# Row-by-row ReLU and row sums rewritten with own semaphores, wide instructions in six blocks, and both stores on one queue

## The chip, the cores and the metric

The kernel runs on one core of one Trainium2 chip. Its time is the device time of one execution in microseconds (us), and medians and means are over executions in the fast state only (all runs here were, or were single looks whose state is called unknown). Each execution also lists the span of the core: from the first to the last instruction of the program that the profile records. The time is longer than the span. The difference I call the *time outside the span*. The run lists give spans to 0.1 us, so a time outside taken from them is good to 0.05 us.

## The reference

```python
# x: float32 [32, 512, 1024]
relu_x = np.maximum(x, 0)
return np.sum(relu_x, axis=-1)        # [32, 512]
```

There are 16,384 rows of 1024 numbers (67.11 MB). Each is clamped at zero and summed, so almost all that moves is the input.

## The kernel before

Each of the 128 partitions owns 128 rows. Seven loads bring 16 rows each, then loads of 8, 4, 2 and 1 rows follow, and the last row comes in four pieces so that little work is left after the last byte. Rows alternate between ScalarE (ReLU with an accumulator) and VectorE (max with zero, then add). The 16-row and 8-row tiles share two buffers. A framework places the semaphores and waits.

```python
chunks = [16] * 7 + [8, 4, 2, 1]            # pieces = [244, 252, 260, 268]
io_pool = ctx.enter_context(tc.tile_pool(name="io", bufs=2))
...
for j, cpd in enumerate(chunks):
    ...                                     # tile xt of cpd rows
    nc.sync.dma_start(out=xt, in_=xv[...])
    for c in range(cpd):
        m = m0 + c
        if m == NT - 2:
            act_op(xt[:, c, :], xt[:, c, :], m)
            nc.scalar.dma_start(out=out2d[:, 0 : NT - 2], in_=res[:, 0 : NT - 2])   # store 1
        elif (c % 2) == 0:
            act_op(xt[:, c, :], xt[:, c, :], m)
        else:
            dve_op(xt[:, c, :], xt[:, c, :], res[:, m : m + 1])
...                                         # four pieces on VectorE
nc.sync.dma_start(out=out2d[:, NT - 2 : NT], in_=res[:, NT - 2 : NT])              # store 2
```

Of the kernel before, what the change touches and what calls it, by code (L numbers as in the profile page):

```python
# [1 line left out]

# [4 lines left out]



EARLY = 1  # L10


def kernel(tc: tile.TileContext, x: bass.AP, out: bass.AP):
    trace_relu_sum(tc, x, out)
    tc.close()
    tc.compile()  # L16
    issue_ahead_of_the_barrier(tc, EARLY)


def issue_ahead_of_the_barrier(tc: tile.TileContext, n_loads: int):  # L20


    SP = mybir.EngineType.SP
    blocks = tc.nc.main_func.blocks
    opening = blocks[0].instructions
    body = next(b for b in blocks if b.name == tc.start_bb_name).instructions
    loads = [i for i in body if i.engine == SP][:n_loads]
    for i in loads:
        assert isinstance(i, mybir.InstDMACopy)
        body.remove(i)  # L30
    at = next(
        n
        for n, i in enumerate(opening)
        if i.engine == SP and isinstance(i, mybir.InstDrain)
    )
    opening[at:at] = loads


@with_exitstack
def trace_relu_sum(  # L40
    ctx: ExitStack,
    tc: tile.TileContext,
    x: bass.AP,
    out: bass.AP,
):
    nc = tc.nc
    fp32 = mybir.dt.float32

    P = nc.NUM_PARTITIONS
    x_flat = x.flatten_outer_dims()  # L50
    N, D = x_flat.shape
    assert N % P == 0
    NT = N // P

    xv = x_flat.rearrange("(p m) d -> p (m d)", p=P)
    out2d = out.rearrange("b s -> (b s)").rearrange("(p m) -> p m", p=P)

    big = 16
    tail = [8, 4, 2, 1]
    pieces = [244, 252, 260, 268]  # L60
    assert sum(pieces) == D
    nbig, rem = divmod(NT - sum(tail) - 1, big)
    assert rem == 0
    chunks = [big] * nbig + tail

    io_pool = ctx.enter_context(tc.tile_pool(name="io", bufs=2))
    res_pool = ctx.enter_context(tc.tile_pool(name="res", bufs=1))
    res = res_pool.tile([P, NT], fp32)

    def act_op(in_ap, out_ap, m):  # L70
        nc.scalar.activation(  # L71
            out=out_ap,
            in_=in_ap,
            func=mybir.ActivationFunctionType.Relu,
            accum_out=res[:, m : m + 1],
        )

    def dve_op(in_ap, out_ap, accum_out):
        nc.vector.tensor_scalar(  # L79
            out=out_ap,  # L80
            in0=in_ap,
            scalar1=0.0,
            scalar2=None,
            op0=mybir.AluOpType.max,
            op1=mybir.AluOpType.add,
            accum_out=accum_out,
        )

    m0 = 0
    for j, cpd in enumerate(chunks):  # L90
        if cpd >= 8:
            xt = io_pool.tile([P, cpd, D], fp32, tag="io", name=f"xt{j}")
        else:
            xt = io_pool.tile([P, cpd, D], fp32, tag=f"t{cpd}", bufs=1, name=f"xt{j}")
        nc.sync.dma_start(  # L95
            out=xt,
            in_=xv[:, m0 * D : (m0 + cpd) * D].rearrange("p (c d) -> p c d", c=cpd),
        )
        for c in range(cpd):
            m = m0 + c  # L100
            if m == NT - 2:
                act_op(xt[:, c, :], xt[:, c, :], m)
                nc.scalar.dma_start(out=out2d[:, 0 : NT - 2], in_=res[:, 0 : NT - 2])
            elif (c % 2) == 0:
                act_op(xt[:, c, :], xt[:, c, :], m)
            else:
                dve_op(xt[:, c, :], xt[:, c, :], res[:, m : m + 1])
        m0 += cpd

    m_last = m0  # L110
    assert m_last == NT - 1
    base = m_last * D
    np_ = len(pieces)
    wlast = pieces[-1] + (np_ - 1)
    ptiles = []
    col = 0
    for i, w in enumerate(pieces):
        shape_w = w if i < np_ - 1 else wlast
        pt = io_pool.tile([P, shape_w], fp32, tag=f"p{i}", bufs=1, name=f"p{i}")
        ptiles.append(pt)  # L120
        nc.sync.dma_start(out=pt[:, 0:w], in_=xv[:, base + col : base + col + w])
        col += w
    last = ptiles[-1]
    for i in range(np_ - 1):
        dve_op(ptiles[i], ptiles[i], last[:, pieces[-1] + i : pieces[-1] + i + 1])
    dve_op(last, last, res[:, m_last : m_last + 1])

    nc.sync.dma_start(out=out2d[:, NT - 2 : NT], in_=res[:, NT - 2 : NT])


# [1 line left out]
_INS = ['x']  # L132
_OUTS = [((32, 512), 'float32')]


# [23 lines left out]
```

## Time and profile before

| what | value | where it is read |
|---|---|---|
| median time, 3 runs | 163.64 us (163.27 to 163.69) | run list |
| span of the profiled run, its time | 161.5 us, 163.31 us | run list |
| load queue, share of 16 DMA engines | 96.9% | page, part 3 |
| VectorE, ScalarE busy | 46%, 43% | page, part 1 |

These are lines of the page of the kernel before, parts 1 and 3. Part 1 gives busy time, share of the span and number of instructions; part 3 gives packets, megabytes and the share of the sixteen DMA engines' span for each queue.

```profile
span 161.5 us, 347 instructions
DVE 74.3 (46%) x134; ACT 69.0 (43%) x129; POOL 0.2 (0%) x4
...
q1 hardware_dynamic: 2304, 67.11, 96.9%
q10 hardware_dynamic: 144, 0.06, 0.1%
q14 instruction: 2, 0.02, 0.0%
```

The load queue q1 is busy almost all of the time and the compute engines are not half busy, so the kernel is bound by the input stream. The queue q10 is ScalarE's store queue.

This is the chain of waits of the kernel before (start, length, what).

```profile
0.78 40.80 DMA xt<-in_x_dram
41.59 0.02 issue
41.61 9.22 DVE xt L79 x16
50.83 0.02 SPq L95
50.85 0.03 issue
50.88 29.41 DMA xt<-in_x_dram
```

The chain seems to say that 9.22 us of VectorE work stand between loads. They do not: the load issued at about 50.9 us queues up behind another one, which is still running and lands only at 60.93 us. A chain follows releases, and a release that comes early is shown all the same. That no time is lost is shown by the landings below, 19.35 us apart.

The end of the kernel before, from the timeline of VectorE and SyncE (start, length, engine, line, operation):

```profile
157.58 0.41 DVE L79 TENSOR_SCALAR_CACHE_REDUCE p<-p 128x244 f32<-128x244 f32 x1 [0.40 <-DMA p<-in_x_dram]
...
158.74 0.43 DVE L79 TENSOR_SCALAR_CACHE_REDUCE p<-p 128x271 f32<-128x271 f32 x1
159.10 0.08 DVE L79 DVE_READ_ACCUMULATOR p<-p 128x1 f32 x1
159.25 0.35 SPq L128 DMA_DIRECT2D out_dram<-res  x1
```

The last piece is reduced at 158.74 us, and store 2 is issued at 159.25 us; the span ends at 161.52 us.

A load is done when all sixteen DMA engines have landed their sixteenth of it. The trace has these landings one by one. The next table is worked out from them, in us; the two 8 KiB instruction packets are at 86.35 and 86.65 us.

| load (before) | first engine | last but one | last |
|---|---|---|---|
| third, 16 rows | 59.97 | 60.84 | 60.93 |
| fourth, 16 rows | 79.35 | 80.20 | 80.29 |
| fifth, 16 rows | 98.70 | 99.63 | 100.13 |
| last piece | 157.27 | 158.12 | 158.60 |

Up to the fourth load the last engine trails the next by 0.09 us. From the fifth on, the first after the instruction packets, it trails by 0.49 us, and keeps this up to the last piece.

### The profile page before, as it was taken

To read this page: it belongs to the slowest core of one execution; us is meant where nothing else is said; L and a number is where in the kernel's file an instruction comes from. 1 tells how busy PE (TensorE), PEld (TensorE's weight loads), DVE (VectorE), ACT (ScalarE), POOL (GpSimd) and SP (SyncE) were. 2 spreads that over 40 slices of the span, in tenths; PEclk is the share of its full clock that TensorE was granted. 3 is DMA by queue.
4 is the path that set the end of the run, shared out by engine and by line. 5 is a ranking of instruction groups with operands and counts; after the bars stand their busy time and mean duration, and the time that the engine had idled before them with its cause. 6 is when DMAs were issued, how large, how long until landed. Compare 5 with 4: busy or idle time off the path is not lost.

```text
span 161.5 us, 347 instructions
## 1 busy us (share of the span) xinstructions
DVE 74.3 (46%) x134; ACT 69.0 (43%) x129; POOL 0.2 (0%) x4
## 2 busy tenths in 40 slices
DVE  0000049700695008940099101991039900598983
ACT  3000049500693008920099001990039700596882
POOL 0000000000000000000000000000000000000000
DMA  8997997996997997997996997997997997999990
GB/s 308 471 503 308 487 487 308 503 503 292 503 503 308 487 503 325 471 519 308 471 519 296 487 503 325 471 503 341 454 503 341 454 503 308 430 438 406 406 359 22
DMA packets 2450, 67.19 MB, mean 416 GB/s; under 512 B 528, under 2 KB 1040, under 8 KB 1168
## 3 DMA queue, kind: packets, MB, share of 16 engines
q1 hardware_dynamic: 2304, 67.11, 96.9%
q10 hardware_dynamic: 144, 0.06, 0.1%
q14 instruction: 2, 0.02, 0.0%
HBM read 67.11 MB, written 0.07 MB: 416 GB/s over the span
## 4 chain that ended last, share of the span: by engine, by line
DMA 79%; DVE 18%; SPq 1%; issue 0%; DVEq 0%
DMA xt<-in_x_dram 62%; DVE xt L79 17%; DMA p<-in_x_dram 17%; SPq L95 1%; DVE p L79 1%; DVEq L79 0%; DVEq L16 0%
## 5 line engine op out<-in xcount | busy, mean ns | idle before, releaser
L79 DVE TENSOR_SCALAR_CACHE_REDUCE xt<-xt 128x1024 f32<-128x1024 f32 x63 | 72.6, 1216 | 84.5 <-DMA xt<-in_x_dram 84.2
L71 ACT ACTIVATE xt<-xt 128x1024 f32<-128x1024 f32 x64 | 66.7, 1043 | 89.0 <-DMA xt<-in_x_dram 89.0
L71 ACT ACTIVATION_READ_ACCUMULATOR xt<-xt 128x1 f32 x64 | 11.9, 187 | 0.0
L79 DVE DVE_READ_ACCUMULATOR xt<-xt 128x1 f32 x63 | 5.2, 83 | 0.0
L79 DVE TENSOR_SCALAR_CACHE_REDUCE p<-p 128x244 f32<-128x244 f32 (+3 forms) x4 | 1.6, 420 | 0.4 <-DMA p<-in_x_dram 0.4
L71 ACT ACT_TABLE_LOAD x1 | 1.3, 1283 | 0.8 <-PEq L143 0.8
L79 DVE DVE_READ_ACCUMULATOR p<-p 128x1 f32 x4 | 0.3, 82 | 0.0
L143 POOL MEMSET const-bfloat16-1.0<- 128x1 bf16 x1 | 0.1, 101 | 0.0
L143 POOL MEMSET const-uint8-127<- 128x1 uint8 x1 | 0.1, 101 | 0.0
L143 POOL MEMSET const-float32-0.0<- 128x1 f32 x1 | 0.1, 98 | 0.2 <-issue 0.2
L143 POOL MEMSET const-float32-1.0<- 128x1 f32 x1 | 0.1, 98 | 0.0
## 6 DMA issues: line engine op xcount, KB each, us to landing
xt<-in_x_dram SPq DMA_DIRECT2D x1, 4096.0 KB, 19.6
xt<-in_x_dram SPq DMA_DIRECT2D x1, 2048.0 KB, 24.2
xt<-in_x_dram SPq DMA_DIRECT2D x1, 1024.0 KB, 26.2
xt<-in_x_dram SPq DMA_DIRECT2D x1, 512.0 KB, 27.0
p<-in_x_dram SPq DMA_DIRECT2D x1, 134.0 KB, 10.0
p<-in_x_dram SPq DMA_DIRECT2D x1, 130.0 KB, 26.5
p<-in_x_dram SPq DMA_DIRECT2D x1, 126.0 KB, 26.7
p<-in_x_dram SPq DMA_DIRECT2D x1, 122.0 KB, 26.8
```

What stands on the lines that cost most here:

```text
L71: nc.scalar.activation(out=out_ap, in_=in_ap, func=mybir.ActivationFunctionType.Relu, accum_out=res[:, m : m + 1],)
L79: nc.vector.tensor_scalar(out=out_ap, in0=in_ap, scalar1=0.0, scalar2=None, op0=mybir.AluOpType.max, op1=mybir.AluOpType.add, accum_out=ac ...
L95: nc.sync.dma_start(out=xt, in_=xv[:, m0 * D : (m0 + cpd) * D].rearrange("p (c d) -> p c d", c=cpd),)
L143: nc = _bacc.Bacc("TRN2", target_bir_lowering=False, num_devices=1)
```

## The change

Its intent: fewer instructions and fewer waits, a deeper queue of loads, and a shorter end. In six of the seven 16-row blocks ScalarE now clamps up to 16 rows in one instruction and VectorE sums them in one. There are three 16-row buffers. The last block and the tail stay row by row. Both stores go out on SyncE's queue. The wait for the last store is put into the closing block, behind the branch to it. The core of the diff (the load, the row instructions, the tail and the pieces are left out):

```diff
-    io_pool = ctx.enter_context(tc.tile_pool(name="io", bufs=2))
+NBUF = 3
+TWO = [[16], [16], [16], [8, 8], [8, 8], [6, 5], []]
+ACT = [0, 0, 0, 0, 0, 5, 8]
+DVE = [0, 0, 0, 0, 0, 0, 8]
...
+    def clamp(ap, loaded):
+        i = nc.scalar.activation(out=ap, in_=ap, func=RELU)
+        ...                                          # waits for its load
+        i.then_inc(sems.act, 1)
+    def total(ap, m, n):
+        nc.vector.tensor_reduce(
+            out=res[:, m : m + n], in_=ap, axis=mybir.AxisListType.X, op=ADD
+        ).wait_op(sems.act, n_act, "sem-ge").then_inc(sems.dve, 1)
...
+        for n in TWO[j]:
+            clamp(buf[:, c : c + n, :], act_waits)
+            total(buf[:, c : c + n, :], m + c, n)
...
-                nc.scalar.dma_start(out=out2d[:, 0 : NT - 2], in_=res[:, 0 : NT - 2])
+    store(0, NT - 2, n_act - 1, n_dve)               # on nc.sync
...
+    nc.cur_bb = nc.bb_map[tc.start_bb_name + "_end"] # the closing block
+    nc.sync.wait_ge(sems.stored, 16 * n_stores)
```

## The prediction

> **What bounds the kernel now.** The input stream. The page gives 67.11 MB read in a span of 161.5 us, the load queue's packets taking 96.9% of the sixteen DMA engines' span, while VectorE is busy 46% and ScalarE 43%. The trace's DMA records show 64 KiB packets of 2.418 us each, back to back: 16 x 65,536 B / 2.418 us = 434 GB/s, which is the 435 GB/s fabric ceiling of the Trainium skill ("DMA: Bandwidth & Descriptors", Where 436 GB/s comes from). Every 16-row load after the first lands 19.35 us after the one before. The chain of waits shows 9.22 us VectorE stretches, but the queue still holds the next load then (a load is issued at 50.8 us; the one before it lands at 60.9), so they cost nothing. Two buffers never starve the queue.
>
> **What the change does to the middle: nothing for time.** From the durations of before (1,039 ns per 1024-element ACTIVATE; VectorE 1,216 ns at 1024 and 414 ns near 257 elements, so about 1.05 ns per element) I estimate 13.8 us for a 16-row clamp and 17.3 us for a 16-row reduce. VectorE is the busiest engine at 17.3 < 19.35 us per load. A buffer comes free about 31 us after landing; with three buffers its next load is needed about 38 us after landing, 7 us of slack. Busy shares rise (VectorE to about 75%, ScalarE to about 65%), the stream stays at 434 GB/s. The last block and the tail are row by row as before.
>
> **What can move: under 1 us.**
> 1. Instruction fetch. The trace shows two 8 KiB packets on the instruction queue at 86.35 and 86.65 us (16 KiB, the block of 256 instructions of the Trainium skill, "Runtime: NRT & Kernel Launch", Instruction fetch mechanics). They hold up one DMA engine: it lands 1.3 us later from then on and becomes the last. Before the fetch the last engine trails the next by 0.09 us, after it by 0.49 us, up to the last piece. Both compute streams are then about 64 records in; the changed ones have about 50 to 60 records in all, against 147 and 143. I expect no fetch in the stream: last landing about 0.48 us earlier.
> 2. The last store is issued at 159.25 us, its wait ends near 160.6, the closing barrier runs 160.8 to 161.5. With the wait behind the branch, the branch hides under the store: 0.1 to 0.2 us.
> 3. Store 1 moves from ScalarE's queue to SyncE's, behind the loads. It needs 0.37 us of issue at about 157.2 us; SyncE is free until 159. Nothing on the critical path.
> 4. VectorE's end (four piece instructions, 157.58 to 159.18) stays.
>
> Sum: about -0.6 us of 163.64 us, all at the end, so I predict 163.0 us, with 162.3 to 163.7 as the range. Chances: faster by over 2% 0.02, within 2% 0.96, slower by over 2% 0.02.
>
> **What would show each step right or wrong.** Right: 16-row loads still 19.35 us apart; DMA share still about 97%; no instruction-queue packets in mid-stream and the last piece landing near 158.1 us; 16-row reduces near 17.3 us; SyncE waiting for buffers without the queue drying. Wrong: a gap between loads; a fetch still there, or one falling near the end; the last VectorE instruction still ending at 159.2 us.
>
> **What would make it wrong.** A 16-row reduce above about 24 us per block would delay loads and cost several us each. A fetch at a worse moment, or a slower start of the first load (its first packets took 2.5 to 3.2 us), moves the result by some tenths. Store 2 queued behind store 1 on one queue may take longer than its 1.4 us.

## The result, and the profile after

| | before | after |
|---|---|---|
| median time, 4 runs each | 163.50 us (163.27 to 163.69) | 163.52 us (163.38 to 163.73) |
| span of the profiled run | 161.52 us | 161.05 us |
| time of that run less its span | 1.8 us | 2.4 us |

The ratio is 1.0003, 95% interval 0.9984 to 1.0022: the same. Ratios are the mean time of one kernel's runs over that of the other's of the same rounds, so not quite the ratio of the medians quoted.

The page of the kernel after, parts 1 and 3:

```profile
span 161.1 us, 160 instructions
DVE 116.9 (73%) x47; ACT 102.8 (64%) x52; POOL 0.2 (0%) x4
...
q1 hardware_dynamic: 2448, 67.18, 97.3%
```

Less than half the instructions are left, the compute engines are busier, and the stream is as busy as before. The q14 line is gone.

Two groups of the page of the kernel after (line, engine, operation, tiles, count, then busy us, mean ns of one, then idle time before them):

```profile
L110 DVE TENSOR_REDUCE res<-io 128x8 f32<-128x8192 f32 (+3 forms) x9 | 97.9, 10931 | 40.5 <-ACT io L102 40.5
L102 ACT ACTIVATE io<-io 128x8192 f32<-128x8192 f32 (+3 forms) x9 | 79.1, 8825 | 47.6 <-DMA io<-in_x_dram 47.6
```

Their means mix four shapes. The timeline of VectorE shows the 16-row form alone:

```profile
36.27 17.22 DVE L110 TENSOR_REDUCE res<-io 128x16 f32<-128x16384 f32 x1 [36.27 <-ACT io L102]
55.59 17.22 DVE L110 TENSOR_REDUCE res<-io 128x16 f32<-128x16384 f32 x1 [2.10 <-ACT io L102]
```

A 16-row sum takes 17.22 us, and the load behind it takes 19.35, so VectorE keeps up. The Trainium skill ("VectorE: DVE Perf Modes", The perf-mode tier table) says that `tensor_reduce` runs at 1x only; this trace does not contradict it, with 17.22 us for 16,384 elements, 1.05 ns each, but no run here has a faster mode beside it to compare.

The end of the kernel after, from the same timeline:

```profile
157.22 0.41 DVE L127 TENSOR_SCALAR_CACHE_REDUCE piece<-piece 128x244 f32<-128x244 f32 x1 [0.43 <-DMA piece<-in_x_dram]
...
158.38 0.43 DVE L193 TENSOR_SCALAR_CACHE_REDUCE piece<-piece 128x271 f32<-128x271 f32 x1
158.74 0.08 DVE L193 DVE_READ_ACCUMULATOR piece<-piece 128x1 f32 x1
```

The last instruction of VectorE starts 0.36 us earlier than before. The landings say why:

| load (after) | first engine | last but one | last |
|---|---|---|---|
| fourth, 16 rows | 79.43 | 80.30 | 80.38 |
| fifth, 16 rows | 98.77 | 99.65 | 99.73 |
| last piece | 157.36 | 158.15 | 158.23 |

The last engine trails by 0.08 us to the end; no engine was held up. The span is 0.47 us shorter, where 0.6 us had been predicted. But the time did not follow it. In all four runs of the kernel after, time less span is 2.33 to 2.38 us. In the profiled run of the kernel before it is 1.8 us, and in the 11 runs of it that the next section's first session lists it is 1.73 to 1.84 us. So 0.5 us were gained inside the span and 0.6 us lost outside it. The trace of the kernel after holds one more clue: an instruction packet of 8 KiB at 163.16 us, 2.1 us behind the last record of the program. The kernel before has none there. (Both traces also hold 8 KiB packets before the span begins, four and six of them. `rows` below has six as well and the time outside of the kernel before, so they are not what differs.)

### The profile page after: what moved, and what is told of

Its sections match the earlier page's. It is cut to its first block, busy times and chain, and to the rows that moved or that the text cites. A ratio compares the mean times of both kernels' runs of the same rounds, so it can differ in the third digit from the quotient of the medians.

```text
span 161.1 us, 160 instructions
## 1 busy us (share of the span) xinstructions
DVE 116.9 (73%) x47; ACT 102.8 (64%) x52; POOL 0.2 (0%) x4
## 3 DMA queue, kind: packets, MB, share of 16 engines
q1 hardware_dynamic: 2448, 67.18, 97.3%
## 4 chain that ended last, share of the span: by engine, by line
DMA 43%; DVE 33%; ACT 17%; another core or an unknown queue 3%; SPq 1%; issue 0%; DVEq 0%
DVE res L110 32%; DMA io<-in_x_dram 25%; DMA piece<-in_x_dram 18%; ACT io L102 17%; SPq L84 1%; DVE piece L127 1%; DVE piece L193 0%; DVEq L29 0%
## 5 line engine op out<-in xcount | busy, mean ns | idle before, releaser
L110 DVE TENSOR_REDUCE res<-io 128x8 f32<-128x8192 f32 (+3 forms) x9 | 97.9, 10931 | 40.5 <-ACT io L102 40.5
L102 ACT ACTIVATE io<-io 128x8192 f32<-128x8192 f32 (+3 forms) x9 | 79.1, 8825 | 47.6 <-DMA io<-in_x_dram 47.6
L117 ACT ACTIVATE io<-io 128x1024 f32<-128x1024 f32 x21 | 21.9, 1044 | 6.8 <-DMA io<-in_x_dram 6.7
L127 DVE TENSOR_SCALAR_CACHE_REDUCE io<-io 128x1024 f32<-128x1024 f32 x15 | 17.4, 1216 | 0.9 <-DMA io<-in_x_dram 0.8
L117 ACT ACTIVATION_READ_ACCUMULATOR io<-io 128x1 f32 x21 | 3.9, 187 | 0.0
L127 DVE TENSOR_SCALAR_CACHE_REDUCE piece<-piece 128x244 f32<-128x244 f32 (+2 forms) x3 | 1.1, 414 | 0.4 <-DMA piece<-in_x_dram 0.4
L127 DVE DVE_READ_ACCUMULATOR io<-io 128x1 f32 x15 | 1.2, 82 | 0.0
```

What stands on the lines that cost most here:

```text
L102: i = nc.scalar.activation(out=ap, in_=ap, func=RELU)
L110: nc.vector.tensor_reduce(out=res[:, m : m + n], in_=ap, axis=mybir.AxisListType.X, op=ADD).wait_op(sems.act, n_act, "sem-ge").then_inc(se ...
L117: i = nc.scalar.activation(out=ap, in_=ap, func=RELU, accum_out=res[:, m : m + 1])
L127: i = nc.vector.tensor_scalar(out=ap, in0=ap, scalar1=0.0, scalar2=None, op0=MAX, op1=ADD, accum_out=accum_out,)
```

## The experiments

Two theories were put against each other.

- **M, the fetch moved.** Every engine reads its instructions in blocks. Before, VectorE and ScalarE each had to fetch a block in mid-stream, and this held up DMA engines that carry the input. Now their programs are so short that the block is first needed in what the runtime runs after the kernel's end, and there the fetch is waited for.
- **R, set-up and closing.** The 0.6 us come from how the new kernel is built: 18 semaphores instead of 10 in all (a text below says 11; the trace shows 10), one store queue less, or the late wait.

The runs that pad a stream do it with waits on a semaphore that has long been reached. They do nothing, and two fit in one instruction. Results of the timed runs, means in us:

| kernel | runs | time | span | time outside | kernel before, same rounds: time, span, outside | 8 KiB packets at |
|---|---|---|---|---|---|---|
| `after_again` | 6 | 163.52 | 161.13 | 2.39 | 163.40, 161.60, 1.80 | 163.28 |
| `pad_act` | 5 | 163.26 | 161.18 | 2.08 | 163.33, 161.55, 1.78 | 122.72 |
| `pad_dve` | 6 | 163.40 | 161.55 | 1.85 | 163.33, 161.55, 1.78 | 142.53 |
| `pad_both` | 6 | 163.28 | 161.48 | 1.79 | 163.33, 161.55, 1.78 | 122.71, 142.22 |
| `rows` | 6 | 163.25 | 161.45 | 1.80 | 163.33, 161.55, 1.78 | 67.29, 67.32 |
| `tail_pads` | 6 | 163.87 | 162.08 | 1.78 | 163.38, 161.61, 1.77 | 160.17, 160.96 |
| `late_pads` | 6 | 163.41 | 161.63 | 1.78 | 163.40, 161.60, 1.80 | 158.87, 159.31 |
| `split_pads` | 6 | 163.67 | 161.88 | 1.79 | 163.45, 161.67, 1.78 | 158.99, 159.60 |

Single looks, so no means: `wait_in_body` 163.71 us (span 161.4, outside 2.31), `act_store` 163.06 (161.0, 2.06), `act_two` 163.46 (161.4, 2.06), `two_bufs` 200.53 (198.1, 2.43). The span of the same kernel varies by some tenths from run to run (161.3 to 161.9 us for the kernel before in one session). The time outside hardly varies (1.73 to 1.84 us in the kernel before, 2.31 to 2.47 in `after_again`), which makes it the sharper measure.

### Padding one stream, then the other, then both

```diff
+        if j == 4:
+            for _ in range(64):
+                nc.scalar.wait_ge(sems.loads[0], 16)     # pad_act, pad_both
+                nc.vector.wait_ge(sems.loads[0], 16)     # pad_dve, pad_both
```

> The changed kernel with 64 waits on a semaphore that is long satisfied, put into ScalarE's stream ahead of its fifth block (it is idle there for some 5 us). The span got 0.47 us shorter by the change (161.52 to 161.05) but the time less the span got 0.55 us longer (1.81 to 2.36 us), and one 8 KiB instruction packet now lies 2.1 us after the last record. Theory M (the fetch moved): ScalarE's instruction block is fetched after the end, and exposed there. With the pads one 8 KiB packet lies in mid-stream (about 100 to 125 us), one DMA engine lands later, the span grows to about 161.2 to 161.6, time less span falls from 2.36 towards 1.8; if it is VectorE's block that counts, nothing of this happens and time less span stays 2.36. Rival R (the 0.55 us comes from how the changed kernel is set up or closed: 18 semaphores instead of 11, one store queue less, the wait behind the branch): time less span stays at 2.36 whatever is padded.

> The same 64 satisfied waits in VectorE's stream instead, ahead of its fifth block; they run in the sequencer while VectorE is still reducing, so no instruction comes later. Theory M: if VectorE's block is the one fetched after the end, an 8 KiB packet appears in mid-stream and time less span falls from 2.36 towards 1.8 us, the span growing by 0 to 0.5 us; otherwise no change. Rival R: 2.36 as in the changed kernel.

> 64 satisfied waits in both streams. Theory M: two 8 KiB packets in mid-stream as in the kernel before (86.35 and 86.65 us there), the last engine trails the next by about 0.5 us from there on, span about 161.5, time less span about 1.8, no instruction packet after the end, time as before within 0.1 us. Rival R: time less span 2.36, and the time then 163.5 plus the 0.4 us that the fetch costs in the stream, 163.9.

Instruction lines of part 3 in the pages of `pad_act` and of `pad_both`:

```profile
q14 instruction: 1, 0.01, 0.0%
```

```profile
q14 instruction: 2, 0.02, 0.0%
```

Padding ScalarE alone brings one packet into the stream, padding VectorE alone brings another one, and padding both brings two. So each engine fetches its own 8 KiB. The time outside the span falls from 2.36 to 2.08, 1.85 and 1.79 us, the last equal to the kernel before. The pads change nothing of semaphores, queues or the closing wait, so R cannot explain this, and M stands. The two packets cost the stream unequal amounts: the mean span with ScalarE's packet is 161.18 us, as without any, with VectorE's it is 161.55. In the trace of `pad_dve` the last engine's lag grows from 0.16 to 0.57 us at its packet, in that of `pad_act` it even shrinks, from 0.29 to 0.21 us: the engine held up was not the last one. Outside the span the two do not add up either: VectorE's left outside costs 0.3 us (`pad_act`), ScalarE's alone 0.07 us (`pad_dve`), both 0.6 us. Why the sum is more than its parts is open. My expectation that time as before would come back with both was met (163.28 against 163.33 us).

What the traces do not show is the fetch behind the end in full. M expects two packets there in the kernel after, and one each in `pad_act` and `pad_dve`; on record is one in the kernel after, and none in the other two. So the cost behind the end rests on the time outside, which the pads move, and what waits there, and for how long, is not shown. The results of all runs were correct.

### The wide instructions undone alone

```diff
-TWO = [[16], [16], [16], [8, 8], [8, 8], [6, 5], []]
-ACT = [0, 0, 0, 0, 0, 5, 8]
-DVE = [0, 0, 0, 0, 0, 0, 8]
+TWO = [[], [], [], [], [], [], []]
+ACT = [8, 8, 8, 8, 8, 8, 8]
+DVE = [8, 8, 8, 8, 8, 8, 8]
         if after:
+            nc.sync.wait_ge(sems.act, after[0])
```

> The changed kernel with every row of the seven blocks processed alone, eight on ScalarE and eight on VectorE (own semaphores, three buffers, both stores on SyncE and the late wait kept): the wide instructions undone alone. Theory M: as many instructions as before, so the fetch is back in mid-stream near 86 us, span about 161.4 to 161.5, time less span about 1.8, time 163.2 to 163.5, so no different from either kernel. Rival R: time less span stays 2.36, time about 163.8 to 163.9.

Page of `rows`, part 1 and the instruction line:

```profile
span 161.4 us, 329 instructions
DVE 74.3 (46%) x134; ACT 69.0 (43%) x129; POOL 0.2 (0%) x4
...
q14 instruction: 2, 0.02, 0.0%
```

With semaphores, buffers, store queue and late wait all new, but row by row, the kernel shows the time outside of the kernel before (1.80 us) and its two packets in mid-stream. Together with the pads this puts the whole shift of 0.6 us down to the number of instructions. The packets came at 67.3 us and not near 86 as expected, so the number of instructions after which an engine fetches is not the same in every program; what else it depends on is open.

### The late wait, the store's queue, and two more instructions

`wait_in_body` puts SyncE's last wait ahead of the branch:

```diff
     n_stores = relu_sum(nc, sems, x, out)
+    nc.sync.wait_ge(sems.stored, 16 * n_stores)
     body.extend(ends)
 ...
-    nc.sync.wait_ge(sems.stored, 16 * n_stores)
```

> The changed kernel with SyncE's last wait ahead of the branch again. If the prediction's 0.1 to 0.2 us for the branch is right, the stretch from the landing of the last store to the end of the span grows from 0.80 us by 0.1 to 0.2 us. If hiding the branch gains nothing it stays at 0.80 us.

Its trace has a record that the kernel after lacks (from the instructions of the closing line: count, duration in ns, start):

```profile
L29 SPq COMPARE_BRANCH  x1: 33/33/33, 160.4 to 160.4; - x1
```

From the landing of store 2 to the end of the span it takes 0.96 us (160.42 to 161.38), against 0.80 us in the kernel after (160.25 to 161.05). So the branch costs 0.16 us when nothing hides it. This is a single look, but in `act_two`, `late_pads`, `split_pads` and `tail_pads` ScalarE's next record also starts 0.156 us after its branch. But the kernel before takes 0.85 us (160.67 to 161.52), not 0.96. The framework had put its closing waits into the closing block, behind the branch, all along. Against the kernel before this part of the change gained 0.05 us: fewer waits, less a slower clearing of the larger number of semaphores at the end (136 ns against 93).

`act_store` gives store 1 back to ScalarE:

```diff
+                if n == 1:
+                    nc.scalar.wait_ge(sems.act, n_act)
+                    nc.scalar.dma_start(out=dst, in_=src).wait_op(sems.dve, n_dve, "sem-ge")...
-    store(0, NT - 2, n_act - 1, n_dve)
```

> The changed kernel with store 1 issued from ScalarE again, ahead of its last row. Theory: nothing on the critical path moves, last VectorE instruction at 158.8 us and span within 0.1 us of 161.05; the second store queue is used again, and if the number of queues were what lengthened the time outside the span, time less span would fall from 2.36 to about 1.8. ScalarE has two or three instructions more, which may bring its fetch forward.

The span is 160.95 us against 161.05, so the store's queue is indeed off the critical path. Time outside fell to 2.06 us, not to 1.8. Either the second queue or the two extra instructions on ScalarE could do that, hence the next run, which adds only instructions:

```diff
     store(NT - 2, 2, n_act, n_dve)
+    for _ in range(5):
+        nc.scalar.wait_ge(arrived[-1], 16)
```

> The changed kernel with two or three satisfied-wait instructions at the end of ScalarE's stream. Store 1 on ScalarE gave 2.06 us of time less span instead of 2.36, either because the second store queue is back or because ScalarE has two instructions more and its fetch starts that much earlier in what follows the end. If it is the instruction count, time less span is about 2.05 to 2.15 here, with both stores on SyncE; if it is the queue, 2.36.

It gave 2.06 us as well, with both stores on SyncE. So the count of instructions is enough, and the queue is not needed. That ScalarE gets to its fetch earlier, while the end is still running, is the likely reason: the packet behind the end starts at 162.71 and 162.70 us, against 163.16 and 163.28 us in the two traces of the kernel after. Both are single looks, but they lie 0.25 us below the lowest of the six runs of `after_again` (2.31 to 2.47 us).

### Two buffers

```diff
-NBUF = 3
+NBUF = 2
         if after:
+            nc.sync.wait_ge(sems.act, after[0])
```

> The changed kernel with two 16-row buffers instead of three (its loads then wait for ScalarE's rows as well). A buffer is held about 31 us after landing (13.9 us clamp, then 17.2 us reduce), longer than the 19.35 us that the other buffer's load lasts, so loads wait: I work out landings of loads 2, 4, 6 near 74, 126 and 171 us and a time near 190 us, DMA share of the span about 82%. If the wide instructions held their buffer for less than 19.35 us, or the third buffer were not needed, the time would stay near 163.5 us.

Page of `two_bufs`: the span, DMA by slices, and the load queue.

```profile
span 198.1 us, 166 instructions
...
DMA  9999999900099999998005999999940999989993
...
q1 hardware_dynamic: 2448, 67.18, 80.0%
```

The zeros are stretches in which no load is under way. With wide instructions a buffer is held for 31.1 us after landing (22.36 to 53.48 us in the kernel after: 13.86 us of clamp, then 17.22 us of sum). One other load of 19.35 us cannot bridge that, but two can. So the third buffer is what makes the wide instructions free, and the middle of the kernel has the slack that the prediction gave it. Loads 2, 4 and 6 (counted from 0) landed at 75.7, 128.7 and 175.5 us instead of 74, 126 and 171: I had left out that a stream that has run dry starts slowly (each engine's first 64 KiB packet took 3.0 to 3.4 us after the first pause and 2.4 to 3.3 us after the other two, instead of 2.42). The time, 200.53 us, missed the expected 190 by 10 us. The late landing of load 6 accounts for 4.5 us; most of the rest was in my sum, because the kernel after takes 22.6 us from that landing to the end of its span and 2.4 us outside, which makes 196 out of 171.

### Looking for a better place for the fetches

If a fetch costs time in the stream and behind the end, a gap between the two might be free: between the last landing and the end of the span. `tail_pads` appends 40 waits to both streams behind their last work:

```diff
     store(NT - 2, 2, n_act, n_dve)
+    for _ in range(40):
+        nc.vector.wait_ge(arrived[-1], 16)
+        nc.scalar.wait_ge(arrived[-1], 16)
```

> The changed kernel with 40 satisfied waits (20 instructions, two waits fit one) appended to the ScalarE and VectorE streams behind their last work, on the last piece's load, so that they run while the last store is on its way. Theory M, sharpened by the pads: each of the two engines fetches one 8 KiB block when it has some 55 to 60 records behind it; the changed kernel ends just before that, and the fetch is then waited for after the end (0.55 us), while a fetch in mid-stream costs the stream 0.3 to 0.5 us. Here both fetches should fall between the last landing and the end (about 158.5 to 161 us), costing neither: span 161.0 to 161.1, time less span 1.75 to 1.85, time about 0.3 to 0.5 us below both kernels. Rival: what a fetch costs after the end it costs in the closing stretch too; span or time less span stays longer by 0.3 us or more, and the time is that of the changed kernel.

Time outside is down to 1.78 us, as M says. But the span grew by 0.95 us against `after_again` (another session; against the kernel before in its own rounds it is 0.47 us longer), and the time by 0.3% (ratio 1.0027, interval 1.0010 to 1.0045). SyncE's wait for the stores in `tail_pads` and in the kernel after (who waited for what: us in total, times, longest):

```profile
SPq L29 <- DMA out_dram<-res: 2.0, 1, 2.0
```

```profile
SPq L29 <- DMA out_dram<-res: 1.1, 1, 1.1
```

In the trace, fifteen parts of store 2 had landed by 160.48 us; the sixteenth landed at 161.44 us. The DMA records show why it was late: ScalarE's packet ran from 160.168 to 160.661 us, and the 8-byte packets of that part start at 160.658, while those of the other fifteen had ended by 160.12. So it seems to have stood behind ScalarE's fetch on one DMA engine (the records do not name the engines; the times meet within 0.003 us). From its packets to its landing another 0.72 us passed, against 0.4 us for the others. The pads have a cost of their own, too: VectorE's last one, with the branch behind it, ended at 161.18 us, so the end would have been late by some 0.7 us (an estimate, from SyncE's 160.5 us without the late part) even with the store on time. This run also shows both sequencers stopping near the fetch, because every wait leaves a record. These are such records (start in us, engine, number in its stream):

```
159.068 ScalarE 63rd        159.782 VectorE 63rd
159.454 ScalarE 64th        160.298 VectorE 64th
```

The waits before and after follow each other in 0.08 and 0.10 us. Both engines pause behind their 63rd record, for 0.39 and 0.52 us, and the packet follows 1.1 to 1.2 us after the 63rd. The pause is over 0.7 us before the packet starts, so it is not the arrival of the block that the engine waits for there. The kernel after, the same program without the pads, has 58 and 54 records in these streams: it ends just short of the mark. The mark is not the same elsewhere: in `rows` the packets came when the engines had begun 45 to 47 records, in `pad_act` 43 and in `pad_dve` 50.

`late_pads` aims both fetches in front of store 2: 13 instructions of padding early in VectorE's stream and four between its third piece and its last, 11 behind ScalarE's last row, all of the late ones waiting for the first piece.

```diff
+        if j == 4:
+            for _ in range(26):
+                nc.vector.wait_ge(sems.loads[0], 16)
 ...
+    for _ in range(7):
+        nc.vector.wait_ge(arrived[0], 16)
+    for _ in range(21):
+        nc.scalar.wait_ge(arrived[0], 16)
     nc.vector.wait_ge(arrived[-1], 16)
```

> Satisfied waits again, but placed so that each engine's 63rd record falls between the first piece's landing (157.2 us) and the last store: 13 instructions in VectorE's stream ahead of its fifth block and four more behind its third piece, eleven in ScalarE's stream behind its last row. With the waits all at the end both fetches came 1.1 us after the 63rd record, at 160.17 and 160.96 us, and the last store's sixteenth part landed 0.96 us late, behind one of them. Theory M with that collision: here the two 8 KiB packets should lie between 158.4 and 159.6 us, behind the load stream and ahead of the last store; then the last landing stays near 158.2 us, store 2 lands near 160.3, span 161.05 to 161.25, time less span 1.75 to 1.85, time 0.3 to 0.5 us under the kernel before and under the changed one. If a fetch costs the same wherever it falls, the time is within 0.1 us of both.

The packets lay where they should and were over (159.73 us) before those of store 2 began (160.05), and its parts landed within 0.22 us of each other. But now VectorE's pause stood in the way. VectorE's waits in `late_pads`:

```profile
DVE piece L200 <- DVE piece L127: 0.4, 1, 0.4
```

Its last instruction began at 158.74 us, 0.36 us later than in the kernel after. The time was 163.41 us, as before (ratio 1.0002, interval 0.9987 to 1.0016).

> The changed kernel unaltered, on the same chip and in the same rounds as the run above, to compare the two and to repeat the split: time less span 2.36 +- 0.05 in every run against 1.78 +- 0.05 of the kernel before, mean span shorter by 0.3 to 0.5 us than that of the kernel before, so a time within 0.3 us of it. If the split was that of one session, it comes out otherwise.

The repeat confirms the split: shorter span by 0.47 us, 0.59 us more outside, and a time within 0.12 us (ratio 1.0008, interval 0.9993 to 1.0023).

`split_pads` leaves out the seven late waits on VectorE, so that its pause falls behind the last instruction.

> In the run before, both fetches lay where they were meant to (158.87 and 159.31 us) and nothing landed late, but VectorE's sequencer stood still from 158.11 to 158.62 us at its 63rd record, between the third piece and the last, and the last instruction began at 158.74 instead of 158.38 us. Here VectorE has the 13 early instructions alone, so that its 63rd record is that of its last instruction and the pause falls under the store; ScalarE keeps its eleven behind the last row. Expected: last VectorE instruction near 158.4 us, VectorE's 8 KiB packet at 159.5 to 160.0 us, store 2 landed by 160.5 us, span 161.05 to 161.3, time less span 1.75 to 1.85, time 0.2 to 0.5 us under the kernel before. If the store waits for the fetch as it did with all waits at the end, its last part lands 0.2 to 0.9 us late and nothing is gained.

VectorE's last instruction did start at 158.48 us, but store 2, issued at 158.95, had its last part at 160.99 us, 0.34 us behind the one before it, and the time was 163.67 us (ratio 1.0013, interval 0.9994 to 1.0031). The DMA records show the same queueing as in `tail_pads`: VectorE's packet ran from 159.603 to 160.050 us, and the last part's own packets start at 160.047, when those of the other parts had ended (159.99). Its landing then came another 0.89 us later, against 0.4 to 0.7 us for the others; that part of the delay stays open. The Trainium skill ("DMA: Bandwidth & Descriptors", Queues, rings and completion order) says that a DMA's semaphore increment lands only after every earlier write from the same DMA engine, across its queues. An increment that lands late behind a fetch on the same engine would fit that, but the traces do not show when the write of a fetch is complete, so no run here shows it.

No placement that I tried beats either kernel by more than the noise, and all three expectations of a gain of 0.2 to 0.5 us were missed. As differences of mean spans from `after_again`, partly across sessions, the fetches cost 0.3 to 0.4 us in the stream (`pad_both`, `pad_dve`, `rows`), 0.5 us with the pause in front of the last instruction (`late_pads`) and 0.7 to 1.0 us beside the last store (`split_pads`, `tail_pads`); behind the end they cost 0.6 us outside the span. None of these places is clearly cheaper than the stream, where the kernel before had them.

## Why the prediction was right or wrong

- **The bound and the middle: right.** Loads stay 19.35 us apart (98.77 to 118.12 us, for one), the load queue's share is 97.3%, and the estimates of 13.8 and 17.3 us for a 16-row clamp and sum were measured as 13.86 and 17.22. Busy shares of 75% and 65% were given, 73% and 64% measured. The 434 GB/s of the stream match the 435 GB/s ceiling of the Trainium skill ("DMA: Bandwidth & Descriptors", Where 436 GB/s comes from): 16 packets of 65,536 B in 2.418 us. The same section says that for transfers between HBM and SBUF the HBM side, about 358 GB/s, is what binds; this one-core stream from HBM ran at 434 and was not held to it.
- **Step 1, the fetch: right within the span, wrong as a gain in time.** The packets left the stream, and the last landing came 0.37 us earlier (158.23 us; the table had started 0.09 us later), against 0.48 predicted. The step that failed is the one that turned "I expect no fetch in the stream" into a gain of time, as if the fetch were gone. It was put off to behind the end, where the time outside grew by 0.6 us. I had read only the span; "one falling near the end" was on my list of wrong signs, but no cost behind the span was in the sum. I also read the two packets as one block of 16 KiB; they are two blocks of 8 KiB, one per engine.
- **Step 2, the branch: mis-sized.** Predicted 0.1 to 0.2 us, measured 0.05. The branch does cost 0.16 us, but the kernel before did not wait ahead of it.
- **Steps 3 and 4, store 1 and VectorE's end: right.** Giving store 1 back to ScalarE moved the span by 0.1 us in a single look, and the four piece instructions keep their length.
- **The sum.** Predicted -0.6 us (163.0), measured 0.0 (median 163.52 against 163.50 us). The range of 162.3 to 163.7 and the forecast of "within 2%" held, but for the size of the gain they held by luck: -0.47 us of span and +0.59 us outside it, in the repeat, cancel.

## What to carry to other kernels

In this kernel, where a stream of loads is the bound and the compute engines have slack, cutting instructions bought nothing in the middle but the fetches (0.3 to 0.4 us); all else was at the ends. So look at time less span as well as at the span, run by run. An instruction fetch is work that a shorter program may move and not remove; here, behind the end of the program, it cost more than in the stream. Before you give a change credit for hiding something, check that the old program did not hide it already, and give wide instructions the buffers that their longer hold needs.

## What the Trainium skill lacked or had wrong

- "Runtime: NRT & Kernel Launch", Instruction fetch mechanics: blocks are said to be of 16 KiB, 256 instructions. In these runs one fetch of one engine is one packet of 8 KiB (`pad_act`, `pad_dve`: one packet each). Whether a setting makes it so here is not shown.
- The same section calls the cost of crossing a block "mostly hidden". Here the sequencer stops for 0.39 us (ScalarE) and 0.52 us (VectorE) in `tail_pads`; in `late_pads` such a stop delays the last VectorE instruction by 0.36 us, and a fetch in the stream leaves one DMA engine up to 0.41 us further behind the others for the rest of the kernel (`pad_dve`: lag 0.16 to 0.57 us).
- No page that I read says that a program that ends just short of a block pays for the fetch behind its end: 2.36 to 2.39 us outside the span instead of 1.78 to 1.80. "Runtime: NRT & Kernel Launch", The launch sequence, lists what the runtime runs there in its preamble and postamble, but the trace has no records of it.
- "Advanced Engine Details and Errata", Control Flow Timing, gives about 51 ns for a branch that is always taken and about 108 ns for a compare-and-branch. The branch to the closing block, recorded as COMPARE_BRANCH with the wait for the stores in the same record, lengthened the end by 0.16 us (0.96 against 0.80 us), with 33 ns in its own record.
- "DMA: Bandwidth & Descriptors" does not give the slow start of a stream: the first 64 KiB packet of each DMA engine took 2.5 to 3.2 us in the kernel before, and 2.4 to 3.4 us after the pauses in `two_bufs`, against 2.42 us in the flow.
